# Position rows spread by SyncE one pair at a time, x in four buffers with its statistics on GpSimd, gate rows laid out by head: a change to a fused mLSTM and sparse-attention block

## The chip, the cores and the metric

The kernel runs on one core of a Trainium2 chip. A core has TensorE (PE), VectorE (DVE), ScalarE (ACT), GpSimd (POOL) and SyncE (SP), which here only issues transfers; 16 DMA engines move the data. The metric is the time of one execution in microseconds (us). Before the change it is 1576.97 us, the median of three runs (1576.12 to 1577.94).

## The reference, cut to what matters

One layer over 1024 positions of width 1024, in float32: a normalization, one input projection, two mixers side by side (an mLSTM with 4 heads of 128 and a sparse attention with 8 heads of 64 in 2 groups), gates that blend their outputs, an output projection, and a gated feed-forward network of width 2816.

```python
u = rms_norm(h, g_norm_mix[l])
proj = jnp.einsum('btd,de->bte', u, w_in[l]) + b_in[l]
mq, mk, mv, mo, mi, mf, nq, nkv, ngate, merge = split_columns(proj, IN_SIZES)
y_m = mlstm_mixer(mq, mk, mv, mo, mi, mf, ...)
y_n = nsa_mixer(nq, nkv, ngate, pe_cmp[l], w_cmp1[l], w_cmp2[l], rel_bias)
branch = jnp.einsum('btnw,nwd->btnd', jnp.stack([y_m, y_n], axis=2), w_branch[l])
h = h + jnp.sum(jax.nn.sigmoid(merge) * branch, axis=2) @ w_out[l]
f = rms_norm(h, g_norm_ffn[l])
h = h + (jax.nn.silu(f @ w_gate[l]) * (f @ w_up[l])) @ w_down[l]
```

`rms_norm` multiplies each row of x by the inverse root of its mean square. The mLSTM's gates `mi`, `mf` (8 columns of the projection) give, for each head and chunk of 128 positions, running sums, maxima and decays. The attention adds to its scores a bias `rel_bias` that depends on the distance between two positions only.

## The kernel before, in words

**Numbers.** Each float32 operand is split into a high part (f32r) and a low part (the rest), and each product is three matmuls: high × high, high × low, low × high (`mm3`, L289 to L292, so PE's rows have lines L290, L291, L292). ACT makes the high parts, VectorE or GpSimd the low ones by a subtraction (`ew`, L443 on GpSimd, L440 on VectorE; `act`, L447; `stt`, L450).

**The planner.** The first stage, to about 400 us, is not written in the order in which it runs. Its steps are given to a planner, `pA`, each with an engine, a cost in ns, the buffers it reads and writes, and sometimes an earliest time (`after`) or a rise in rank (`boost`). It builds one fixed order per engine ahead of the launch. The engines keep to their order and wait for each other by semaphores. So a changed cost can move many later instructions. SyncE issues its transfers in that order; each waits at its head of the queue until its buffers are free and until the eighth transfer before it has landed.

**The start (0 to 60 us).** x is loaded in eight tiles of 128 rows, in the order 0, 2, 4, 6, 1, 3, 5, 7 (XO), by `load_x` (L489) into slots of the buffer XR, three of them, x0 to x2; the fourth, x3, takes the junk output of ACT's Square. `norm` (L507) handles tile 0 alone and then the tiles in pairs, (2, 4), (6, 1), (3, 5) and 7: ACT squares and sums the row (L510), DVE forms mean plus epsilon (L511), ACT the root (L512), DVE the reciprocal and one Newton step of four operations (L516 to L520), and then DVE scales the tile (`stt`, L450, XR<-XR,MSC,PSA). `trans` transposes it on PE (L541) into UTH and UTL, and `p0` (L562) makes the first projection with the weights p0h, p0l (288 columns: values of the attention, into VT and VHA, and the gates, into GT, by a copy on GpSimd, L587). Meanwhile GpSimd loads rows of b_in into MSC, and stores the rows of bias by distance, d_row (8 heads of 1920 numbers).

**The pairs (60 to 330 us).** Twelve pairs of weight blocks (PAIRS, L720) are each multiplied by one level of Strassen's method, seven products instead of eight, in the order q = 1, 2, 6, 7, 5, 4, 3 (QO, L719). Weight blocks come by SyncE into rA and Rg; `prep` (L770) makes the sums of blocks (DVE L440, and rA, Rg as targets) and splits them into wOwhi and wOwlo; `product` (L864) is PE's part (PSA<-UTH,wOwhi and so on); `finish` (L802) adds products and bias into rows (DVE L450, RG or Rg), and `store` sends those to DRAM by SyncE (d_q<-Rg, d_kc<-Rg, 256 KB each). Rg and RG are used again and again, so a store must land before DVE writes its buffer anew. In front of the pairs stand `gates` (L945: maxima and decays of the mLSTM, small DVE and ACT operations, two transposes by way of DRAM, d_M and d_S, issued by GpSimd), and then eight loads on GpSimd's queue (L1144 and L1145), one for each attention head: each spreads one row of d_row over 128 rows of d_rep, from DRAM to DRAM, 960 KB. The attention reads d_rep only after 400 us. Their due times, 110 us and 14 us more for each, are the planner's; nothing on the chip holds them back.

**The mLSTM heads (280 to 400 us).** `head_load` (L1100) brings for each head the mask M, q, k, v, gate o and S into buffers, `values` (L1113) transposes v on PE (L1122), `core` (L1195) does the chunks.

**The branches (740 to 780 us).** For each of 8 column blocks two products with w_branch (L290 to L292, br<-YH,whi). The first weights are split on ACT (whi, L261) and DVE (wlo, L269). The sigmoid of the merge gates (L1866) is ACT's too, with a table load ahead of it. The inputs YH, YL are made tile by tile: DVE adds two halves (`split_y`, L1836), ACT and DVE split (L286, L287). FIRST (L1884) lists the first eight products; after the first, the second weight is split.

The rest, attention, output projection and feed-forward network (400 to 1578 us otherwise), is not touched.

Of the kernel before, what the change touches and what calls it, by code (L numbers as in the profile page):

```python
# [174 lines left out]
def body(ctx, tc, a, out, stop=None, dbg=None):  # L175
# [166 lines left out]
    with ExitStack() as sa:  # L342
# [119 lines left out]
        sq_A = K(sqA, keys=[("x3", 0)])  # L462
# [40 lines left out]
        def norm(*ii):  # L503
# [4 lines left out]
            for i in ii:  # L508
                sb_[i] = s
                stp("ACT", 1250.0, lambda i=i: nc.scalar.activation(sqA, flat(xb[i].ap), AF.Square, accum_out=stA[:, XO.index(i), 0:1]), [xb[i]], [s, sq_A])  # L510
            stp("DVE", 160.0, lambda: nc.vector.tensor_scalar(st[:, :, 0:1], st[:, :, 0:1], 1.0 / D, EPS, ALU.mult, ALU.add), (), [s])  # L511
            stp("ACT", 210.0, lambda: nc.scalar.activation(st[:, :, 1:2], st[:, :, 0:1], AF.Sqrt), tabs[-1:], [s])  # L512

            def newton():
# [5 lines left out]
                nc.vector.tensor_tensor(y, y, t, ALU.mult)  # L520
# [41 lines left out]
        def p0(i):  # L562
# [38 lines left out]
        def fsplit(q, j, src, reads):  # L601
# [168 lines left out]
        def prep(m, q):  # L770
# [150 lines left out]
        for n, i in enumerate(XO[4:]):  # L921
# [1614 lines left out]
```

## Time and profile before

| | us |
|---|---|
| median of three runs | 1576.97 |
| the profiled execution | 1580.19 |
| its span, first to last instruction | 1578.4 |
| PE busy | 1536.5 |
| DVE busy | 1153.7 |
| ACT busy | 793.3 |
| POOL busy | 174.4 |

The mean granted clock of TensorE was 0.989 of full speed. DMA moved 205.86 MB in 169979 packets. Rows of a timeline give the start in us, the duration, the engine (SPq is SyncE issuing a transfer), the line, the operation, output<-input, the shapes, how many were alike, and in brackets the idle time before with what ended it. Rows of waits give the engine and line that waited, the engine, buffer and line that released it, the us in all, the times and the longest. Rows of windows give start:end, length, the busy time of one or of each engine with its count of instructions, the granted clock, and what DMA did. The row PEclk gives the clock in tenths for 40 slices of the span.

### The profile page before, as it was taken

What the parts mean: (1) busy time and instruction counts of PE and PEld (TensorE: products, weight loads), DVE (VectorE), ACT (ScalarE), POOL (GpSimd) and SP (SyncE); (2) the same over time, 40 slices, a digit from 0 to 9 for tenths busy, and PEclk for the clock granted to TensorE, in tenths of its full rate; (3) what the DMA queues carried; (4) which work ended last, traced back from release to release, by engine and by line L of the source; (5) the groups of instructions that cost most, each with busy time, mean ns of one, the idle gap of its engine ahead of it and who ended that gap; (6) DMA issues with size and microseconds to landing.
All of it is one profiled execution on the core that took longest, in us unless ns stands there. A gap on an engine that the chain in (4) does not pass through costs nothing.

```text
span 1578.4 us, 22429 instructions
## 1 busy us (share of the span) xinstructions
PE 1536.5 (97%) x7810; PEld 1300.7 (82%) x7810; DVE 1153.7 (73%) x2380; ACT 793.3 (50%) x1713; POOL 174.4 (11%) x291
## 2 busy tenths in 40 slices
PE   9896999999999999999999999999999999999997
PEld 7775888888899989888788888888888888888886
DVE  5966788745798868784655677666666666988996
ACT  5533454457588868784444453333333333454443
POOL 4410001323111311002002000000000000000130
PEclk9997999999999999999999999999999999999999
DMA  6567455789523543216457324322222223750302
GB/s 201 170 185 225 125 173 166 201 259 190 179 53 103 99 111 71 83 48 236 144 161 226 107 81 134 94 80 81 81 87 87 80 80 113 274 193 22 107 0 107
DMA packets 169979, 205.86 MB, mean 130 GB/s; under 512 B 10345, under 2 KB 128391, under 8 KB 169610
## 3 DMA queue, kind: packets, MB, share of 16 engines
q1 hardware_dynamic: 156584, 179.43, 36.3%
q0 software_dynamic: 12992, 24.67, 6.8%
q8 instruction: 61, 1.00, 0.3%
q14 instruction: 52, 0.43, 0.1%
q10 hardware_dynamic: 290, 0.33, 0.1%
HBM read 149.77 MB, written 62.48 MB: 134 GB/s over the span
## 4 chain that ended last, share of the span: by engine, by line
PE 89%; DMA 5%; DVE 3%; ACT 1%; issue 1%; SPq 0%; POOL 0%; DVEq 0%; ACTq 0%; POOLq 0%
PE PS L291 14%; PE PS L290 14%; PE PS L292 14%; PE PSA L292 6%; PE PSA L290 6%; PE PSA L291 6%; PE T L1519 4%; PE d L290 3%; PE d L292 3%; PE d L291 3%; PE obank L1539 2%; PE obank L1541 2%; DMA d_q<-Rg 2%; PE br L292 2%; PE br L291 2%; PE br L290 2%
## 5 line engine op out<-in xcount | busy, mean ns | idle before, releaser
L1968 DVE TENSOR_TENSOR sl<-PS,sl 128x512 f32<-128x512 f32 x182 | 123.5, 688 | 100.9 <-PE PS L292 100.5
L1528 DVE TENSOR_TENSOR TL<-T,TH 128x512 fp32r<-128x512 f32 (+1 forms) x184 | 103.2, 581 | 32.5 <-ACT TH L1524 31.4
L1524 ACT ACTIVATE TH<-T 128x512 fp32r<-128x512 f32 (+1 forms) x184 | 90.1, 510 | 29.4 <-PE T L1519 26.8
L1968 DVE TENSOR_TENSOR sl<-sl,sl 128x512 f32<-128x512 f32 (+1 forms) x130 | 88.4, 687 | 22.0 <-DMA d_h<-sl 7.4
L292 PE MATMUL PSA<-UTH,wOwlo 128*128 128x512 f32 x164 | 65.2, 397 | 15.0 <-DVE wOwlo L440 15.0
L1971 ACT ACTIVATE sl<-sl 128x512 f32<-128x512 f32 (+1 forms) x77 | 48.6, 632 | 57.9 <-PE PS L291 34.4
L1968 POOL TENSOR_TENSOR acc<-acc 128x512 f32<-128x512 f32 x6 | 9.2, 1546 | 617.7 <-DVE acc L1968 617.6
L1539 PE MATMUL obank<-TH,VHL 128*128 128x256 f32 x264 | 75.4, 309 | 1.4 <-DMA VHL<-d_vh 1.4
L290 PE MATMUL d<-UTH,whi 128*128 128x512 f32 x176 | 71.9, 409 | 1.0 <-ACT mg L1355 0.7
L292 PE MATMUL d<-UTH,wlo 128*128 128x512 f32 x176 | 69.1, 393 | 0.0
L291 PE MATMUL d<-UTL,whi 128*128 128x512 f32 x176 | 69.0, 392 | 0.0
L1541 PE MATMUL obank<-TL,VHL 128*128 128x256 f32 x264 | 68.0, 281 | 0.0
L290 PE MATMUL PS<-q 128*128 128x512 f32 x172 | 66.9, 389 | 0.0
L291 PE MATMUL PS<-q 128*128 128x512 f32 x172 | 66.9, 389 | 0.0
L292 PE MATMUL PS<-q 128*128 128x512 f32 x172 | 66.9, 389 | 0.0
L1971 ACT ACTIVATE q<-sl 128x512 fp32r<-128x512 f32 x74 | 43.1, 623 | 42.3 <-PE PS L291 32.2
L290 PE MATMUL PSA<-UTH,wOwhi 128*128 128x512 f32 x156 | 63.4, 406 | 0.0
L291 PE MATMUL PSA<-UTL,wOwhi 128*128 128x512 f32 x156 | 60.8, 390 | 0.0
L1971 ACT ACTIVATE wh<-sl 128x512 fp32r<-128x512 f32 x39 | 24.6, 631 | 58.2 <-PE PS L291 40.8
L290 PE MATMUL br<-YH,whi 128*128 128x512 f32 x128 | 50.5, 395 | 2.2 <-ACT whi L261 2.2
L1539 PEld LDWEIGHTS obank<-TH,VHL 128*128 128x128 f32 x264 | 49.8, 189 | 2.6 <-ACT TH L1524 1.6
L292 PE MATMUL br<-YH,wlo 128*128 128x512 f32 x128 | 50.5, 395 | 0.5 <-DVE wlo L269 0.5
(1381 smaller groups left out, 4944.9 us busy)
## 6 DMA issues: line engine op xcount, KB each, us to landing
d_gu<-sl SPq DMA_DIRECT2D x44, 256.0 KB, 2.2
rA<-in_w_in SPq DMA_DIRECT2D x18, 512.0 KB, 5.9
q<-d_mg SPq DMA_DIRECT2D x32, 256.0 KB, 3.6
d_rep<-d_row POOLq DMA_DIRECT2D x8, 960.0 KB, 19.1
sl<-in_w_down SPq DMA_DIRECT2D x15, 512.0 KB, 3.4
sl<-d_gu SPq DMA_DIRECT2D x15, 512.0 KB, 4.7
ra<-in_w_gate SPq DMA_DIRECT2D x14, 512.0 KB, 3.8
ra<-in_w_up SPq DMA_DIRECT2D x13, 512.0 KB, 4.8
```

Source lines behind the costliest of these rows:

```text
L290: nc.tensor.matmul(ps, ah, bh, start=first, stop=False)
L291: nc.tensor.matmul(ps, ah, bl, start=False, stop=False)
L292: nc.tensor.matmul(ps, al, bh, start=False, stop=last)
L1519: nc.tensor.transpose(pt[:, z, P * r:P * r + P], e, ident)
L1524: nc.scalar.activation(hl[0][:, 0:m], pt[:, 0:m], AF.Copy)
L1528: nc.vector.tensor_tensor(hl[1][:, 0:m], pt[:, 0:m], cast32(hl[0])[:, 0:m], ALU.subtract)
L1539: nc.tensor.matmul(po, vv, th[:, z, :], start=(st[1] == 0), stop=False)
L1541: nc.tensor.matmul(po, vv, tl[:, z, :], start=False, stop=(st[1] == st[2]))
L1968: return pl.step(alts, lambda e: ENG[e].tensor_tensor(out_(), x(), y(), alu), reads, writes, **kw)
L1971: return pl.step((("ACT", cost),), lambda e: nc.scalar.activation(out_(), x(), fn), reads, writes, **kw)
```

## The change

**Broadcasts.** The eight loads of d_rep leave GpSimd's queue. SyncE issues one for each of the pairs m = 2 to 9, as a step behind the product (m, 7), and it counts as a reader of that product's weights, so the planner can't put it earlier than these are made.

**x and its statistics.** x has four slots, with two loads ahead instead of one; the junk output of Square goes to a PSUM bank, in two halves of 512 (for tile 0 still to x3). The mean (one small operation for tile 0, two otherwise) and the Newton step go to GpSimd; DVE keeps the reciprocal.

**Small shifts.** The low part of VHA is always GpSimd's, and that of the forms for q = 4, 5 may be; the first eight instead of four preps have a higher rank; one merge piece moves from x3 to x0.

**Layout by head.** Gate rows, maxima and decays are kept in the order head, chunk instead of chunk, head. The loads of M and S then read one contiguous row of 1024 numbers per head instead of eight pieces of 128. One copy of 32 numbers is added to `carry`.

**Heads and branches.** For heads 1 to 3, v is loaded first, then M, q, k. In the branch stage both first weights are fetched and split ahead of the first product, and the third is loaded there.

The diff, cut to its core (index changes of the layout by head are left out where they repeat):

```diff
         def load_x(i):
-            xb[i] = slot(f"x{XO.index(i) % 3}")
+            xb[i] = slot(f"x{XO.index(i) % 4}")
             load("SP", 512, [(lambda: flat(xb[i].ap), a["x"][P * i:P * i + P, :])], (), [xb[i]])
...
                 sb_[i] = s
-                stp("ACT", 1250.0, lambda i=i: nc.scalar.activation(sqA, flat(xb[i].ap), AF.Square, accum_out=stA[:, XO.index(i), 0:1]), [xb[i]], [s, sq_A])
-            stp("DVE", 160.0, lambda: nc.vector.tensor_scalar(st[:, :, 0:1], st[:, :, 0:1], 1.0 / D, EPS, ALU.mult, ALU.add), (), [s])
-            stp("ACT", 210.0, lambda: nc.scalar.activation(st[:, :, 1:2], st[:, :, 0:1], AF.Sqrt), tabs[-1:], [s])
+                if n == 0:
+                    junk = K(None, keys=[("x3", 0)], make=lambda: XR[:, 3, 0:512].bitcast(mybir.dt.bfloat16))
+                    stp("ACT", 1250.0, lambda i=i: nc.scalar.activation(junk.ap, flat(xb[i].ap), AF.Square, accum_out=st[:, 0, 0:1]), [xb[i]], [s, junk])
+                    continue
+                for z in range(2):
+                    junk = K()
+                    stp("ACT", 780.0, lambda i=i, z=z, junk=junk: nc.scalar.activation(junk.ap, xb[i].ap[:, z, :], AF.Square, accum_out=stA[:, XO.index(i), 3 * z:3 * z + 1]), [xb[i]], [s, junk])
+            y, v, g, w = (st[:, :, c:c + 1] for c in (2, 0, 3, 1))
+
+            def mean():
+                if n:
+                    nc.gpsimd.tensor_tensor(v, v, g, ALU.add)
+                nc.gpsimd.tensor_scalar(v, v, 1.0 / D, EPS, ALU.mult, ALU.add)
 
             def newton():
-                y, v, t = (st[:, :, n:n + 1] for n in (2, 0, 3))
-                nc.vector.reciprocal(y, st[:, :, 1:2])
-                nc.vector.tensor_tensor(t, y, y, ALU.mult)
-                nc.vector.tensor_tensor(t, t, v, ALU.mult)
-                nc.vector.tensor_scalar(t, t, -0.5, 1.5, ALU.mult, ALU.add)
-                nc.vector.tensor_tensor(y, y, t, ALU.mult)
-            stp("DVE", 950.0, newton, (), [s])
+                nc.gpsimd.tensor_tensor(g, y, y, ALU.mult)
+                nc.gpsimd.tensor_tensor(g, g, v, ALU.mult)
+                nc.gpsimd.tensor_scalar(g, g, -0.5, 1.5, ALU.mult, ALU.add)
+                nc.gpsimd.tensor_tensor(y, y, g, ALU.mult)
+            stp("Pool", 320.0, mean, (), [s])
+            stp("ACT", 210.0, lambda: nc.scalar.activation(w, v, AF.Sqrt), tabs[-1:], [s])
+            stp("DVE", 160.0, lambda: nc.vector.reciprocal(y, w), (), [s])
+            stp("Pool", 640.0, newton, (), [s])
...
-            if n + 3 < NT:
-                load_x(XO[n + 3])
+            if n + 4 < NT:
+                load_x(XO[n + 4])
...
         load_x(XO[3])
+        load_x(XO[4])
...
-            ew((("DVE", 430.0), ("Pool", 1000.0)), lambda: VHA[:, i, :, 64:128], lambda: vt, lambda: cast32(VHA)[:, i, :, 0:64], ALU.subtract, [vb], [hb])
+            ew((("Pool", 1100.0),), lambda: VHA[:, i, :, 64:128], lambda: vt, lambda: cast32(VHA)[:, i, :, 0:64], ALU.subtract, [vb], [hb])
...
-            ew(ANY if j < 2 else V, lambda: lo, src, lambda: cast32(hi), ALU.subtract, reads, [b])
+            ew(ANY if j < 2 or q in (4, 5) else V, lambda: lo, src, lambda: cast32(hi), ALU.subtract, reads, [b])
...
-            pA.boost = PB_ if nop[0] <= 4 else 0
+            pA.boost = PB_ if nop[0] <= 8 else 0
...
-            merge_half(0, z, mA, ("x3 g21".split()[z], 1), lambda n, z=z: [x for i in range(4 * z, 4 * z + 4) for x in (ub[i][0::2] if n >= 4 else ub[i][1::2])], fill=False)
+            merge_half(0, z, mA, ("x0 g21".split()[z], 1), lambda n, z=z: [x for i in range(4 * z, 4 * z + 4) for x in (ub[i][0::2] if n >= 4 else ub[i][1::2])], fill=False)
...
-            D_(200.0, lambda: nc.vector.tensor_copy(gif[:, 0], GT[:, :, 24:28]))
+            D_(200.0, lambda: nc.vector.tensor_copy(gif[:, 0].rearrange("p h c -> p c h"), GT[:, :, 24:28]))
...
-            P_(lambda: nc.tensor.transpose(pc.ap[0:32, 0:1], mp[:, 0:8, :].rearrange("p c h -> p (c h)"), ident[0:1, 0:1]), pc)
+                    nc.vector.tensor_tensor_scan(mp[:, h, 1:9], rw[:, 8 * h:8 * h + 8], rw[:, 32 + 8 * h:40 + 8 * h], 0.0, ALU.max, ALU.add)
+                nc.vector.tensor_copy(rw[:, 0:32].rearrange("p (h c) -> p h c", h=MH), mp[:, :, 0:8])
+            D2(1100.0, carry, pr)
+            P_(lambda: nc.tensor.transpose(pc.ap[0:32, 0:1], rw[:, 0:32], ident[0:1, 0:1]), pc)
 
             def maxima():
...
                 if key in "MS":
-                    r0 = (d_M if key == "M" else d_S)[h:h + 1, :]
-                    src = bass.AP(tensor=r0.tensor, offset=r0.offset, ap=[[0, P], [4 * P, NT], [1, P]])
-                    load("SP", 512, [(lambda b=b: v8c(b), src)], [b_MS], [b], cost=600.0)
+                    r0 = (d_M if key == "M" else d_S)[8 * h:8 * h + 1, :]
+                    src = bass.AP(tensor=r0.tensor, offset=r0.offset, ap=[[0, P], [1, T]])
+                    load("SP", 512, [(lambda b=b: flat(b.ap), src)], [b_MS], [b], cost=600.0)
...
-        for h in range(NH):
-            load("Pool", 983, [(d_rep[h], d_row[h, :].partition_broadcast(P))], (), [K(True)], cost=700.0, after=110000.0 + 14000.0 * h)
...
             product(m, q)
+            if q == 7 and 1 < m < NP - 2:
+                load("SP", 983, [(d_rep[m - 2], d_row[m - 2, :].partition_broadcast(P))], [OB[m, q]], [K(True)], cost=700.0)
...
-        head_load(1, "Mqkv")
+        head_load(1, "vMqk")
...
         for half in range(2):
             load_gates(1, half)
+        for d in range(2):
+            W[d] = ws.get(j_br[d])
+        ws.dma(j_br[2])
         for n, (d, half, b) in enumerate(FIRST):
-            if b == 0 and half == 0:
-                W[d] = ws.get(j_br[d])
             x = branch(d, half, b)
             if n == 0:
-                ws.split(j_br[1])
-                ws.dma(j_br[2])
                 gate(d, half, b, *x)
                 split_y(6)
                 continue```

SyncE's queue behind the gates, at pair 2, before (d_q, d_kc and d_mq are stores of results, rA, Rg and VW targets of loads):

```order
L416 DMA d_q_102<-RG_200 128x4x128
L416 DMA d_q_101<-RG_200 128x4x128
L416 DMA Rg_764<-in_w_in 128x4x256
L416 DMA d_kc_96<-RG_200 512x1x128
L416 DMA rA_206<-in_w_in 128x4x128 x2
L416 DMA d_kc_95<-RG_200 512x1x128
L416 DMA VW<-d_kc_95 64x1024
L416 DMA VW<-d_kc_95 64x1023
L416 DMA VW<-d_kc_95 64x1024
L416 DMA VW<-d_kc_95 64x1023
L416 DMA rA_207<-in_w_in 128x4x128 x2
```

and now:

```order
L415 DMA d_q_102<-RG_200 128x4x128
L415 DMA d_rep_84<-d_row 128x1920
L415 DMA d_q_101<-RG_200 128x4x128
L415 DMA Rg_791<-in_w_in 128x4x256
L415 DMA d_kc_96<-RG_200 512x1x128
L415 DMA d_kc_95<-RG_200 512x1x128
L415 DMA rA_206<-in_w_in 128x4x128 x2
L415 DMA VW<-d_kc_95 64x1024
L415 DMA VW<-d_kc_95 64x1023
L415 DMA VW<-d_kc_95 64x1024
L415 DMA VW<-d_kc_95 64x1023
L415 DMA d_rep_85<-d_row 128x1920
```

The first broadcast stands between two stores of d_q and the second ahead of the next weight loads; the other six follow 7 to 18 transfers apart.

GpSimd's queue at the start now (MSC holds the statistics, p0l the low part of the first weights, RG the raw ones):

```order
L520 TENSOR_SCALAR MSC<-MSC 128x1
L523 TENSOR_TENSOR MSC<-MSC 128x1
L524 TENSOR_TENSOR MSC<-MSC 128x1
L525 TENSOR_SCALAR MSC<-MSC 128x1
L526 TENSOR_TENSOR MSC<-MSC 128x1
L566 TENSOR_TENSOR p0l<-RG_200,p0h 128x576 x2
L415 DMA MSC<-in_b_in 128x128
L415 DMA MSC<-in_b_in 128x152
L415 DMA MSC<-in_b_in 128x8
L519 TENSOR_TENSOR MSC<-MSC 128x2
L520 TENSOR_SCALAR MSC<-MSC 128x2
L415 DMA d_row<-ewwlo_211 8x480
```

Before, p0l was GpSimd's first arithmetic, and the three loads of b_in were followed by two stores of d_row; now tile 0's statistics stand ahead of p0l, and the mean of the pair (2, 4) behind the loads.

ACT's queue at the first branch products, before (q are gates and halves of y, d a merge gate's product, whi the second weight's high part):

```order
L1355 ACTIVATE q_5_0_7735<-d_1_7880,COLS 128x512
L1866 ACT_TABLE_LOAD
L1866 ACTIVATE q_3_4_7747<-q_3_4_7747 128x512
L261 ACTIVATE whi_7934<-raw_7835 128x1024
L286 ACTIVATE YH<-q_0_2_7745 128x512 x2
```

and now:

```order
L1366 ACTIVATE q_5_0_7757<-d_1_7902,COLS 128x512
L261 ACTIVATE whi_7942<-raw_7857 128x1024
L1877 ACT_TABLE_LOAD
L1877 ACTIVATE q_3_4_7769<-q_3_4_7769 128x512
L286 ACTIVATE YH<-q_0_2_7767 128x512 x2
```

The split of the second weight has moved from behind the table load and the first sigmoid to ahead of both.

More of the change, by code (lines that the diff above doesn't have):

```diff
@@ L360, in body @@
         stA = MSC[:, 680:712].rearrange("p (i c) -> p i c", i=NT)
-        gif = MSC[:, 712:776].rearrange("p (z c h) -> p z c h", z=2, c=NT)
+        gif = MSC[:, 712:776].rearrange("p (z h c) -> p z h c", z=2, c=NT)
         rw = MSC[0:1, 776:840]
-        mp = MSC[0:1, 840:876].rearrange("p (c h) -> p c h", c=9)
+        mp = MSC[0:1, 840:876].rearrange("p (h c) -> p h c", c=9)
         stage = RG0.rearrange("p (k c) -> p k c", k=KT)
@@ L461, in body @@
         GPRIOR = {"0": b_st, "1": b_p0h, "2": b_p0l}
-        sq_A = K(sqA, keys=[("x3", 0)])
         xform, b_rr, b_vh = [], [], []
@@ L965, in gates @@
             pg, pr, pc, pq = (K() for _ in range(4))
-            D_(200.0, lambda: nc.vector.tensor_copy(gif[:, 0], GT[:, :, 24:28]))
+            D_(200.0, lambda: nc.vector.tensor_copy(gif[:, 0].rearrange("p h c -> p c h"), GT[:, :, 24:28]))
             pA.todo["DVE"][-1].deps |= set(b_GT.w) | {b_rows[7].w[0]}
-            D_(200.0, lambda: nc.vector.tensor_tensor(gif[:, 1], GT[:, :, 28:32], BF[:, None, :].to_broadcast([P, NT, MH]), ALU.add))
+            D_(200.0, lambda: nc.vector.tensor_tensor(gif[:, 1].rearrange("p h c -> p c h"), GT[:, :, 28:32], BF[:, None, :].to_broadcast([P, NT, MH]), ALU.add))
             for z in range(2):
-                P_(lambda z=z: nc.tensor.transpose(pg.ap[0:32, P * z:P * z + P], gif[:, z].rearrange("p c h -> p (c h)"), ident), pg)
+                P_(lambda z=z: nc.tensor.transpose(pg.ap[0:32, P * z:P * z + P], gif[:, z].rearrange("p h c -> p (h c)"), ident), pg)
             iT, fT = t(), t()
@@ L1000, in carry @@
                 nc.vector.tensor_copy(rw, pr.ap[0:1, 0:64])
-                nc.vector.memset(mp[:, 0, :], 0.0)
+                nc.vector.memset(mp[:, :, 0:1], 0.0)
                 for h in range(MH):
-                    nc.vector.tensor_tensor_scan(mp[:, 1:9, h], rw[:, h:32:4], rw[:, 32 + h:64:4], 0.0, ALU.max, ALU.add)
-            D2(1000.0, carry, pr)
-            P_(lambda: nc.tensor.transpose(pc.ap[0:32, 0:1], mp[:, 0:8, :].rearrange("p c h -> p (c h)"), ident[0:1, 0:1]), pc)
+                    nc.vector.tensor_tensor_scan(mp[:, h, 1:9], rw[:, 8 * h:8 * h + 8], rw[:, 32 + 8 * h:40 + 8 * h], 0.0, ALU.max, ALU.add)
+                nc.vector.tensor_copy(rw[:, 0:32].rearrange("p (h c) -> p h c", h=MH), mp[:, :, 0:8])
+            D2(1100.0, carry, pr)
+            P_(lambda: nc.tensor.transpose(pc.ap[0:32, 0:1], rw[:, 0:32], ident[0:1, 0:1]), pc)
             def maxima():
@@ L1211, in st_a @@
                 E_, PT[c], KW[c] = take("E"), take("PT"), take("KW")
-                stp("ACT", 400.0, lambda: nc.scalar.activation(E_.ap, v8(MB)[:, c, :], AF.Exp, bias=GCOL[:, 4 * c + h:4 * c + h + 1]), [MB, b_gc, tabs[-1]], [E_])
+                stp("ACT", 400.0, lambda: nc.scalar.activation(E_.ap, v8(MB)[:, c, :], AF.Exp, bias=GCOL[:, 8 * h + c:8 * h + c + 1]), [MB, b_gc, tabs[-1]], [E_])
                 stp("DVE", 290.0, lambda: nc.vector.tensor_tensor(PT[c].ap, pa_.ap[:, 0:128], E_.ap, ALU.mult), [pa_, E_], [PT[c]])
@@ L1234, in st_b @@
                     else:
-                        stt(350.0, lambda: CN.ap, lambda: CN.ap, DEC[:, 4 * c + h:4 * c + h + 1], lambda: o(pu), ALU.mult, ALU.add, [pu, b_dec], [CN])
+                        stt(350.0, lambda: CN.ap, lambda: CN.ap, DEC[:, 8 * h + c:8 * h + c + 1], lambda: o(pu), ALU.mult, ALU.add, [pu, b_dec], [CN])
                 stp("ACT", 290.0, lambda: nc.scalar.activation(nd[:, c, :], o(pn), AF.Copy), [pn], [ndb])
@@ L1255, in norm_1 @@
                 nc.vector.scalar_tensor_tensor(t0, den, -1.0, den, ALU.mult, ALU.max)
-                nc.vector.tensor_tensor(t0, t0, ECOL[:, h:32:4], ALU.max)
+                nc.vector.tensor_tensor(t0, t0, ECOL[:, 8 * h:8 * h + 8], ALU.max)
                 nc.vector.reciprocal(t0, t0)
@@ L1301, in body @@
         core(0)
-        head_load(2, "Mqkv")
+        head_load(2, "vMqk")
         mask(2)
@@ L1308, in body @@
         core(1)
-        head_load(3, "Mqkv")
+        head_load(3, "vMqk")
         mask(3)
```

1 line of the change is left out of this document (removed).

## The prediction

> **What bounds the kernel now.** I read the page of the profile first: the busy shares and the row of granted clocks.
>
> ```profile
> PE 1536.5 (97%) x7810; PEld 1300.7 (82%) x7810; DVE 1153.7 (73%) x2380; ACT 793.3 (50%) x1713; POOL 174.4 (11%) x291
> ...
> PEclk9997999999999999999999999999999999999999
> ```
>
> TensorE (PE) is busy for 1536.5 of 1578.4 us, and the change takes no matmul away. All it can win is the 41.9 us in which PE is idle, and the time in which PE runs at a lowered clock (the 7, slice 4, 118 to 158 us, is such a place). So next I read what PE waited for in four windows: 0 to 50 us, 50 to 140, 330 to 450 and 740 to 765. Each row gives the us in all, the count and the longest.
>
> ```profile
> PE PSA L541 <- DVE XR L450: 4.7, 1, 4.7
> ...
> PE PSA L292 <- DVE wOwlo L440: 15.8, 2, 15.0
> ...
> PE PSA L1122 <- DMA XB<-d_mv: 2.9, 1, 2.9
> ...
> PE br L290 <- ACT whi L261: 2.2, 1, 2.2
> PE br L292 <- DVE wlo L269: 0.5, 1, 0.5
> ```
>
> One wait of 15.0 us is over a third of all idle time. The change touches all of these places, and I take them one by one.
>
> **The stall at 115 us: eight broadcasts d_rep.** The queues of GpSimd and SyncE, VectorE's and PE's timelines, the busy times in VectorE's gap, and the DMA queues and issues from 98 to 131 us:
>
> ```profile
> 98.16 3.59 POOL L416 DMA_DIRECT2D d_rep<-d_row  x7
> ...
> 100.09 1.50 SPq L416 DMA_DIRECT2D d_q<-Rg  x2
> ...
> 128.96 0.75 DVE L450 SCALAR_TENSOR_TENSOR Rg<-PSA,COLS,XR 128x512 f32<-128x512 f32 x1 [21.71 <-DMA d_q<-Rg]
> ...
> 130.36 0.79 PE L292 MATMUL PSA<-UTH,wOwlo 128*128 128x512 f32 x1 [14.98 <-DVE wOwlo L440]
> ...
> 107.26:128.96 21.70, 8.12 (x36) 6.38 (x34) 0.00 (x1) 0.00 (x1) 0.00 (x0) 0.77 1.01 308
> ...
> q0 software_dynamic: 1232, 7.88, 77.3%
> ...
> d_q<-Rg SPq DMA_DIRECT2D x2, 256.0 KB, 17.5
> ```
>
> GpSimd issues seven broadcasts within 3.6 us. From then on their queue fills 77.3% of 16 engines for 33 us: 0.773 × 33 / 8 = 3.2 us of all engines for each. Behind them two stores of 256 KB, issued from 100.1 on, take 17.5 us. VectorE must not write Rg again before its store has landed; it comes for it at 128.96 - 21.71 = 107.25 and stands still. PE works on for 8.1 us (the window's first number after its length), runs dry, and waits 14.98 us. After that it works at half clock (us; PE busy; clock; DMA share; GB/s):
>
> ```profile
> 130.40:136.00 5.60, 5.60 (x13) 0.50 1.03 323
> 136.00:141.60 5.60, 5.60 (x26) 1.00 0.59 147
> ```
>
> 13 matmuls in 5.6 us and then 26 in the next 5.6: 2.8 us more are lost.
>
> In the changed program no broadcast stands in GpSimd's queue here. SyncE issues the first behind those stores, and the others one a pair, 7 to 18 of its transfers apart. So the store should take what an undisturbed one of its size takes:
>
> ```profile
> d_gu<-sl SPq DMA_DIRECT2D x44, 256.0 KB, 2.2
> ```
>
> Issued at 100.1 to 101.6, it lands by 104, before VectorE wants Rg. What is late next? Nothing that the rows show: in the gap VectorE, ACT and GpSimd did nothing at all, and a shorter wait is covered by PE's 8.1 us of lead. I take 14.98 + 2.8 = **17.8 us** gained; bounds 15 (the clock falls anyway) and 18.6 (the small waits of that window go too, 15.8 in all).
>
> **What the broadcasts cost where they go.** PE, PEld, DVE, ACT, POOL, clock, DMA share and GB/s from 140 to 330 us, and PE, clock, share and GB/s in the fullest part:
>
> ```profile
> 140.00:330.00 190.00, 190.00 (x880) 158.36 (x879) 147.41 (x204) 86.47 (x144) 23.95 (x30) 1.00 0.60 168
> ...
> 280.00:320.00 40.00, 40.00 (x178) 1.00 0.84 217
> ```
>
> PE never waits there, and on average 40% of DMA time is free. One broadcast every 20 us or so adds 3.2 / 20 = 0.16 to the share, which just fits even at 0.84. Behind each on SyncE's own queue stand the next stores and weight loads. How much delay such a store bears can be read off the stall: issued at 101, wanted at 107.25, usual time 2.2, so 4 us spare, and PE's lead of 8.1 after that: 12 us against 3.2. I cost the eight at **0**. A gain is excluded, since PE has no wait to lose there; the bounds are 0 and 8 × 3.2 = 25.6 (rival c).
>
> [...]
>
> **The start: four x buffers, statistics on GpSimd.** PE, ACT, DVE and POOL before 60 us:
>
> ```profile
> 24.86 0.38 PE L290 MATMUL PSA<-p0h,UTH 128*128 128x288 f32 x1
> ...
> 31.55 2.63 PE L541 MATMUL PSA<-cst,XR 128*128 128x128 f32 x16
> 33.93 0.38 PE L290 MATMUL PSA<-p0h,UTH 128*128 128x288 f32 x1
> ...
> 45.66 3.67 PE L541 MATMUL PSA<-cst,XR 128*128 128x128 f32 x16 [4.68 <-DVE XR L450]
> ...
> 56.20 0.60 PE L541 MATMUL PSA<-cst,XR 128*128 128x128 f32 x4
> ...
> 40.57 1.06 ACT L510 ACTIVATE XR<-XR 128x1024 bf16<-128x1024 f32 x1 [2.91 <-DMA XR<-in_x]
> ...
> 19.75 0.17 DVE L520 TENSOR_TENSOR MSC<-MSC 128x2 f32<-128x2 f32 x1
> 19.95 1.41 DVE L450 SCALAR_TENSOR_TENSOR XR<-XR,MSC,PSA 128x512 f32<-128x512 f32 x2
> ...
> 18.60 1.65 POOL L416 DMA_DIRECT2D MSC<-in_b_in  x3
> ...
> 23.15 0.21 POOL L587 COPY GT<-VT 128x32 f32<-128x32 f32 x1 [1.07 <-DVE VT L586]
> ...
> 58.38 0.49 POOL L587 COPY GT<-VT 128x32 f32<-128x32 f32 x1
> ```
>
> Gain: with three buffers x5 arrives late, ACT's Square of it waits until 40.57, and PE waits 4.68 us for x3 and x5, which are normalized together. With a fourth buffer, and the loads ahead of a weight load, this wait goes. Loss: x2 and x4 are normalized later. Their mean now stands on GpSimd behind three DMA issues that end at 20.25, after which come 2 + 4 small GpSimd operations, a root on ACT, a reciprocal on DVE and four changes of engine. Small GpSimd arithmetic isn't in the trace of before; its nearest rows are the 128x32 copies, 0.21 us and, when the engines are full, 0.49. I take 0.21, the row nearest in time: 6 × 0.21 + 2 × 0.17 (root and reciprocal, by VectorE's row at 19.75) + 4 × 0.25 (my estimate of a change of engine) = 2.6. So scaling starts at 22.8 rather than 19.95, and allowing 0.4 us that PE fills, x2's projection at 27.3 rather than 24.86. From there I lay PE's rows end to end. Two projections take 6.7 (24.86 to 31.55): x4's ends at 34.0. About 1.3 us idle before x6's transposes, since its scaling moves as well, and 2.63 + 0.7 for these: 38.6 (33.93 before). x6's and x1's projections took from 33.93 to 40.98 (45.66 - 4.68), 7.05: 45.65. Then, without a wait, 2.63 for the transposes of x3 and x5 and 6.7 for their projections: 55.0, where before stands 56.20: **+1.2**. The new idle time may bring a half-clock stretch, which cost 2.8 above; I don't count on one, since PE's longest new idle time is 1.3 us. Bounds: six operations at 0.49 for each of two more pairs, exposed, 2 × 1.7 = 3.4 worse: -3; the wait of 4.7 won with the lag hidden: +5.
>
> Lower parts that go from VectorE to GpSimd (VHA, some forms) unload the engine that PE waited for at 45.66; 0. The layout by head adds one copy of 32 elements off PE's path; 0.
>
> **Head 1's v.** SyncE's queue, landing times, PE's timeline and the chain of waits at 330 us:
>
> ```profile
> 326.14 0.58 SPq L416 DMA_DIRECT2D XB<-d_M  x1
> ...
> XB<-d_M SPq DMA_DIRECT2D x1, 512.0 KB, 7.4
> ...
> 331.00 0.27 PE L1209 MATMUL PSA<-cst,VW 128*128 128x128 f32 x1
> ...
> 327.98 10.33 DMA XB<-d_mv
> ...
> 338.44 1.06 PE PSA L1122 x8
> ```
>
> v was issued fourth, at 327.98, and took 10.33. Now it is first, at about 326.1, where d_M took 7.4. A store of half its size takes 2.2, so 4.4 would be the least; I take the middle, 5.9: landing at 332.0. PE's order also asks for v earlier, in place of the block that ends at 331.1, so 0.9 to 1.0 of the 2.9 remains: **+1.9**; bounds 0.5 and 2.9.
>
> **The branch stage.** ACT, DVE and PE's clock at 755 us:
>
> ```profile
> 752.55 1.28 ACT L1866 ACT_TABLE_LOAD   x1 [3.95 <-DMA q<-d_mg]
> ...
> 754.38 1.04 ACT L261 ACTIVATE whi<-raw 128x1024 fp32r<-128x1024 f32 x1
> ...
> 760.92 1.22 DVE L1836 TENSOR_TENSOR q<-q 128x1024 f32<-128x1024 f32 x1
> ...
> 757.20:760.60 3.40, 3.40 (x10) 0.50 0.55 163
> ```
>
> The second weight's split on ACT stood behind a table load that waits for the gates until 752.55; now it stands ahead of it, in ACT's 3.95 us of idle time. That wins 2.16 (its row above, 2.2) + 0.53 and the half clock of 757.2 to 760.6, 1.7. Next to be late is the last tile of y, whose sum (760.92) is still behind the first two gates: with PE some 3 us earlier I put the new wait at 0.9. **+3.5**; bounds 1.8 (the clock falls all the same) and 4.4.
>
> **Sum.** 17.8 + 0 + 1.2 + 1.9 + 3.5 = 24.4 us. The span of 1578.4 becomes 1554.0. The profiled execution, 1580.2, is 1.8 above its span and 3.2 above the median of the runs shown (1576.97), and the gain is taken off that median: 1552.6.
>
> **Rivals.**
> (a) The start turns out worse: GpSimd's small operations at 0.49, -3 for +1.2: 1556.8. With one or two broadcasts exposed as well, 3.2 to 6.4: 1560 to 1563. For it: the row of 58.38. Against: GpSimd is 11% busy.
> (b) Half the stall stays. Not the broadcasts alone, but SyncE's own loads and stores hold the store up: it lands late, VectorE waits, and 8.9 of 17.8 are won: 1561.5. Against: to cost PE anything the store would have to land after 115, 14 us after its issue.
> (c) Slower: the broadcasts stand in the one queue that brings weights and takes results away. If each holds back what the next products need by all its 3.2 us, and PE idles each time, 25.6 are lost: 1578.2; with half clock after each wait (8 × 1.7), 1591.8. It decides from 24.4 / 8 = 3.05 us exposed a pair. For it: the share of 0.84 at the end. Against: the 12 us of slack and lead. [...]
> (d) The start wins its whole wait: +5 for +1.2, and the last 0.9 in the branch stage: 1547.9.
> (e) The change doesn't do as it says, and the planner bunches the broadcasts again: SyncE's order shows them apart, so no chance.
>
> **Chances.** The forecast, 1549 to 1556.5: 0.6; (a) 0.17; (b) 0.08; (c) 0.06; (d) 0.09. The range reaches to the far side of (d) and through (a) to (b): 1547 to 1564. A measurement of this kernel can tell about 0.2%, 3.2 us, from no change. Faster 0.93: all but (c) and a little of (b). Within it 0.03: (c) at the strength that just eats the gain. Slower 0.04: (c) in full.
>
> **What would show it.** Right: VectorE without a wait on d_q from 100 to 130 us; PE busy at full clock from 60 to 330 us; broadcasts that land in 4 to 9 us each; no wait of 4.7 at x3's transposes, but x2's projection 2 to 3 us later; whi ahead of the table load. Wrong: PE waits for weights or stores next to a d_rep, or half clock after 140 us (c); GpSimd's statistics at 0.5 us, PE idle from 20 to 40 us (a); VectorE waiting on Rg at 107 us again (b).

## The result

The changed kernel takes 1555.86 us, the median of four runs (1554.76 to 1556.88), beside 1577.45 for the kernel before in the same comparison (four runs, 1576.12 to 1578.2): 21.6 us less. The ratio is 0.9864, with a 95% interval of 0.9847 to 0.9881, which is 18.8 to 24.1 us. The profiled execution took 1556.88 with a span of 1555.1, so by the two spans (1578.4 before) the gain is 23.3.

The page of the profile after, busy shares and granted clock:

```profile
PE 1533.9 (99%) x7810; PEld 1299.3 (84%) x7810; DVE 1149.2 (74%) x2351; ACT 793.7 (51%) x1724; POOL 191.9 (12%) x330
...
PEclk8999999999999999999999999999999999999999
```

PE's idle time went from 41.9 to 21.2 us. Its busy time fell by 2.6 us with the same 7810 matmuls, as less of it runs at half clock: the 7 in the row of clocks is gone, and the mean clock is 0.995, where it was 0.989. PE's waits over the whole span, us in all, times, longest:

```profile
PE PSA L550 <- ACT VHA L446: 1.7, 1, 1.7
PE PSA L550 <- DVE XR L449: 1.3, 1, 1.3
PE PSA L292 <- DVE wOwhi L439: 1.2, 1, 1.2
PE obank L1550 <- DMA VHL<-d_vh: 1.2, 1, 1.2
PE PSA L580 <- ACT p0h L446: 1.2, 2, 0.9
PE PSA L498 <- DVE MSC L367: 1.1, 1, 1.1
PE PSA L290 <- ACT wOwhi L446: 0.8, 1, 0.8
...
PE br L290 <- ACT YH L286: 0.6, 1, 0.6
```

The waits of 15.0, 4.7, 2.9 and 2.2 us are gone; nothing longer than 1.7 has come. The first two rows stand at new places, and the third and seventh (1.2 and 0.8, at 75 to 78 us) are new. DMA from 98 to 131 us, where the broadcasts had filled the engines: queues, and issues with KB and us to landing:

```profile
q1 hardware_dynamic: 8499, 7.14, 79.9%
q0 software_dynamic: 144, 0.05, 3.0%
...
d_rep<-d_row SPq DMA_DIRECT2D x2, 960.0 KB, 6.5
...
d_q<-RG SPq DMA_DIRECT2D x4, 256.0 KB, 4.0
d_q<-Rg SPq DMA_DIRECT2D x2, 256.0 KB, 3.6
```

The stores of d_q land in 3.6 to 4.0 us instead of 17.5 (not the 2.2 that I took, but before VectorE wants their buffers: it no longer waits for a store between 100 and 135 us), and two of the eight broadcasts fall into this window instead of all.

To see where the time went I follow four landmarks on PE that both programs have: x7's transposes (56.20 before), the first transposes of head 0's v, the first attention product, and the first and last branch product. Before:

```profile
L1122 PE MATMUL PSA<-cst,Rg x16: 271/272/273, 328.6 to 361.1; 128*128 128x128 f32 x16
...
L1539 PE MATMUL obank<-TH,VHL x264: 275/282/387, 415.6 to 723.0; 128*128 128x256 f32 x132
...
L290 PE MATMUL br<-YH,whi x128: 389/389/628, 747.7 to 838.9; 128*128 128x512 f32 x128
```

and after (each row gives ns min/median/max and the first and last start):

```profile
54.14 0.39 PE L290 MATMUL PSA<-UTH,wOwhi 128*128 128x512 f32 x1
...
55.52 0.60 PE L550 MATMUL PSA<-cst,XR 128*128 128x128 f32 x4
...
L1133 PE MATMUL PSA<-cst,Rg x16: 271/272/273, 311.4 to 342.9; 128*128 128x128 f32 x16
...
L1550 PE MATMUL obank<-TH,VHL x264: 277/282/387, 395.6 to 703.0; 128*128 128x256 f32 x132
...
L290 PE MATMUL br<-YH,whi x128: 389/389/502, 727.7 to 815.6; 128*128 128x512 f32 x128
```

| stretch | before | after | difference | forecast |
|---|---|---|---|---|
| start, to x7's transposes | 56.2 | 55.5 | -0.7 | -1.2 |
| pairs, to head 0's v | 272.4 | 255.9 | -16.5 | -17.8 |
| heads, to the first attention product | 87.0 | 84.2 | -2.8 | -1.9 |
| attention, to the first branch product | 332.1 | 332.1 | 0 | 0 |
| branch products | 91.2 | 87.9 | -3.3 | -3.5 |
| the rest | 739.5 | 739.5 | 0 | 0 |

The first landmark has moved in PE's order. Six matmuls of the first pair, 1.4 us (54.14 to 55.52), now run ahead of x7's transposes; before, none did. By equal work the start has gained 2.1 us and the pairs 15.1.

### The profile page after: what moved, and what is told of

Same layout as the page of the kernel before. It is cut to its first block, busy times and chain, and to the rows that moved or that the text cites. A ratio compares the mean times of both kernels' runs of the same rounds, so it can differ in the third digit from the quotient of the medians.

```text
span 1555.1 us, 22464 instructions
## 1 busy us (share of the span) xinstructions
PE 1533.9 (99%) x7810; PEld 1299.3 (84%) x7810; DVE 1149.2 (74%) x2351; ACT 793.7 (51%) x1724; POOL 191.9 (12%) x330
## 4 chain that ended last, share of the span: by engine, by line
PE 90%; DVE 4%; DMA 3%; ACT 1%; issue 1%; POOL 0%; SPq 0%; DVEq 0%; POOLq 0%; ACTq 0%
PE PS L291 15%; PE PS L290 15%; PE PS L292 15%; PE PSA L290 6%; PE PSA L292 6%; PE PSA L291 6%; PE T L1530 4%; PE d L290 2%; PE obank L1550 2%; PE d L292 2%; PE d L291 2%; PE obank L1552 2%; PE br L291 2%; PE br L292 2%; PE br L290 2%; DVE acc L1978 1%
## 5 line engine op out<-in xcount | busy, mean ns | idle before, releaser
L1539 DVE TENSOR_TENSOR TL<-T,TH 128x512 fp32r<-128x512 f32 (+1 forms) x184 | 103.1, 581 | 32.5 <-ACT TH L1535 31.4
L1550 PE MATMUL obank<-TH,VHL 128*128 128x256 f32 x264 | 75.5, 309 | 1.2 <-DMA VHL<-d_vh 1.2
L290 PE MATMUL d<-UTH,whi 128*128 128x512 f32 x176 | 71.9, 409 | 1.0 <-ACT mg L1366 0.7
L292 PE MATMUL d<-UTH,wlo 128*128 128x512 f32 x176 | 69.1, 393 | 0.0
L290 PE MATMUL PS<-q 128*128 128x512 f32 x172 | 66.9, 389 | 0.0
L292 PE MATMUL PS<-q 128*128 128x512 f32 x172 | 66.9, 389 | 0.0
L290 PE MATMUL PSA<-UTH,wOwhi 128*128 128x512 f32 x156 | 64.6, 414 | 0.8 <-ACT wOwhi L446 0.8
L292 PE MATMUL PSA<-UTH,wOwlo 128*128 128x512 f32 x164 | 64.1, 391 | 0.0
L267 POOL TENSOR_TENSOR wlo<-raw,whi 128x256 fp32r<-128x256 f32 x44 | 32.1, 759 | 168.6 <-ACT whi L261 138.3
L1550 PEld LDWEIGHTS obank<-TH,VHL 128*128 128x128 f32 x264 | 49.8, 189 | 2.4 <-ACT E1c L1479 1.4
L1552 PEld LDWEIGHTS obank<-TL,VHL 128*128 128x128 f32 x264 | 50.0, 189 | 1.1 <-DVE TL L1539 0.3
## 6 DMA issues: line engine op xcount, KB each, us to landing
d_gu<-sl SPq DMA_DIRECT2D x44, 256.0 KB, 2.2
q<-d_mg SPq DMA_DIRECT2D x32, 256.0 KB, 3.1
```

The costliest lines, as they stand in the source:

```text
L267: nc.gpsimd.tensor_tensor(lo[:, zs], v[:, zs], cast32(hi)[:, zs], ALU.subtract)
L290: nc.tensor.matmul(ps, ah, bh, start=first, stop=False)
L292: nc.tensor.matmul(ps, al, bh, start=False, stop=last)
L1539: nc.vector.tensor_tensor(hl[1][:, 0:m], pt[:, 0:m], cast32(hl[0])[:, 0:m], ALU.subtract)
L1550: nc.tensor.matmul(po, vv, th[:, z, :], start=(st[1] == 0), stop=False)
L1552: nc.tensor.matmul(po, vv, tl[:, z, :], start=False, stop=(st[1] == st[2]))
```

## The experiments

My theory: the stall came from eight broadcasts in flight at once, and one at a time is hidden; the places are independent. Rivals: it is the queue that counts, not the spacing; a broadcast on SyncE's queue costs something each time; the start is no gain. Ratios are to the kernel before in the same session; its median there was 1580.1 to 1580.9 (1575.3 to 1584.9).

**Broadcasts back on GpSimd, all else as in the changed kernel.**

```diff
-            if q == 7 and 1 < m < NP - 2:
-                load("SP", 983, [(d_rep[m - 2], ...)], [OB[m, q]], [K(True)], cost=700.0)
+        for h in range(NH):
+            load("Pool", 983, [(d_rep[h], ...)], (), [K(True)], cost=700.0, after=110000.0 + 14000.0 * h)
```

> The changed kernel with only the eight broadcasts back on GpSimd's queue, all issued behind the gates. Theory (the stall comes from eight broadcasts in flight at once): VectorE waits some 20 us on a store of d_q again, PE idles 13 to 16 us near 115 us, and the time is 1555.9 + 16 to 18 = 1572 to 1574. Rival (the stall went because the planner reordered the work around it, not because of the broadcasts): no such wait, within 3 us of 1555.9.

1572.59 us, ratio 0.996 (0.9943 to 0.9977). The stall is back: PE's waits from 60 to 160 us, and VectorE's.

```profile
PE PSA L292 <- DVE wOwlo L439: 15.1, 1, 15.1
PE PSA L292 <- DVE wOwhi L439: 1.2, 1, 1.2
PE PSA L290 <- ACT wOwhi L446: 0.8, 1, 0.8
```

```profile
DVE RG L449 <- DMA d_q<-RG: 22.5, 1, 22.5
```

This time it is the buffer RG rather than Rg, of a later store, with the same effect. The stretch of the pairs takes 271.3 us (324.3 less 52.96), 15.4 more than in the changed kernel. So the new order of the work around it is not what removed the stall.

**Only the spread, in the kernel before.** The edit is the reverse, on the kernel before.

> The kernel before with only the broadcasts moved to SyncE, one a pair; start, heads and branches as before. Theory: the gain of the whole change less the start (0.7), heads (2.8) and branches (3.3): 1577.5 - 16 to 18 = 1559.5 to 1561.5, with the waits of 4.7 at x3, 2.9 at head 1's v and 2.7 in the branches still there. Rival (the spread needs the earlier start and the new ranks to be hidden): PE waits beside a broadcast after 130 us, 1564 or more.

1562.53 us (1 us above the range expected), ratio 0.9906 (0.9875 to 0.9937); by the interval 10 to 20 us faster. PE's waits, up to 60 us and at the heads:

```profile
PE PSA L541 <- DVE XR L450: 3.9, 1, 3.9
...
PE PSA L1122 <- DMA XB<-d_mv: 2.7, 1, 2.7
```

Start and heads wait as before, and no wait stands beside a broadcast. The pairs take 255.3 us (307.8 less 52.47), 17.1 less than before: the spread does it alone.

**The same spacing on GpSimd's queue.** The planner's claim that a broadcast reads the product's weights makes no semaphore, since the transfer doesn't read them; on GpSimd's queue, which is otherwise empty from 103 to 246 us, it would pace nothing. So a copy that does read them stands ahead of each:

```diff
             if q == 7 and 1 < m < NP - 2:
-                load("SP", 983, ...)
+                stp("Pool", 150.0, lambda m=m, o=OB[m, q]: nc.gpsimd.tensor_copy(PACE[0:1, m:m + 1], cast32(o.ap[:, 0, :])[0:1, 0:1]), [OB[m, q]], [K(True)])
+                load("Pool", 983, ...)
```

> The changed kernel with the broadcasts on GpSimd's queue, but paced: ahead of each stands a copy of one number that reads the weights of the product (m, 7), so GpSimd issues it only when these are made. Theory (only the spacing counts, not the queue): no stall, 1555.9 within 2 us. Rival (a queue of its own is what hurts, since its packets take turns with SyncE's): waits of a store of some us beside each broadcast, 1560 to 1572. Second rival (SyncE's one ring costs something in the changed kernel): 1 to 5 us faster, 1551 to 1555.

1555.59 us (1553.61 to 1556.04), ratio 0.9853 (0.983 to 0.9876): as the changed kernel. That the packets of two queues take turns is in the trace of the kernel before: from 104 to 126 us, 988 packets of GpSimd's queue (6.74 MB) and 979 of SyncE's (0.49 MB) ran. At this spacing that costs nothing that can be measured. GpSimd's issues, the first two, and the landing of all eight:

```profile
112.43 0.55 POOL L416 DMA_DIRECT2D d_rep<-d_row  x1
131.06 0.52 POOL L416 DMA_DIRECT2D d_rep<-d_row  x1
```

```profile
d_rep<-d_row POOLq DMA_DIRECT2D x8, 960.0 KB, 5.0
```

The pairs take 255.8 us against 255.9. At this spacing it makes no difference whether a broadcast lands in 5.0 us on a queue of its own or in 6.9 (all eight) on SyncE's. What the change got from SyncE's queue is the pace, without an instruction for it.

**All eight at one place on SyncE's queue.** The step of the change, with all eight broadcasts behind the product (2, 7).

> The changed kernel with all eight broadcasts on SyncE's queue at pair 2, between three transfers of results, instead of one a pair. Theory (bunching is the cause in any queue, and in one ring the transfers behind have to wait for all of them): 8 x 3.2 = 25.6 us of transfers ahead of the next loads and stores, less some 12 us of slack and lead: PE idle 12 to 20 us, 1568 to 1579. Rival (SyncE's queue protects the stores by its order): 1556 to 1559.

1561.1 us, ratio 0.9897 (0.9869 to 0.9924). Neither number came out: the pairs take 260.4 us (315.1 less 54.69), only 4.5 more than spread. SyncE's queue and PE's waits from 100 to 140 us:

```profile
109.44 0.92 SPq L415 DMA_DIRECT2D d_q<-RG  x2
110.52 1.86 SPq L415 DMA_DIRECT2D d_rep<-d_row  x3
112.49 0.65 SPq L415 DMA_DIRECT2D d_q<-RG  x1
113.18 1.25 SPq L415 DMA_DIRECT2D d_rep<-d_row  x2
115.91 0.57 SPq L415 DMA_DIRECT2D d_kc<-RG  x1
116.53 5.36 SPq L415 DMA_DIRECT2D d_rep<-d_row  x3
124.93 0.39 SPq L415 DMA_DIRECT2D Rg<-in_w_in  x1
```

```profile
PE PSA L290 <- ACT wOwhi L446: 2.2, 1, 2.2
PE PSA L292 <- DVE wOwhi L439: 0.7, 1, 0.7
```

The stores ahead of them are safe, and what was pushed back (the next weights, issued at 124.9 rather than 117.6) costs PE 2.9 us of waits and some half clock behind them (a clock of 0.91 from 120 to 140 us). So bunching costs 15 us where the broadcasts start at 98 to 100 us, ahead of stores that are wanted 6 us after their issue, and 4.5 where they start at 110, behind most of these. Whether it is SyncE's queue or the place that helped is not told apart by these runs.

**Each broadcast twice, and four times.**

```diff
-                load("SP", 983, [(d_rep[m - 2], d_row[m - 2, :].partition_broadcast(P))], ...)
+                load("SP", 983, [(d_, d_row[m - 2, :].partition_broadcast(P)) for d_ in (d_rep[m - 2], *d_more[m - 2])], ...)
```

> The changed kernel with each broadcast issued twice on SyncE, the second into memory that nobody reads. Theory (a broadcast is covered by the slack of some 12 us): 3.2 us more of DMA time a pair, 114 + 51 of 190 us, so no wait of PE: 1555.9 within 1.5. Rival (the transfers behind are on the path): up to 8 x 3.2 = 25.6 more, and at least 5: 1561 to 1581.

1555.24 us, ratio 0.9839 (0.9822 to 0.9856): nothing.

> The changed kernel with each broadcast issued four times. From 140 to 330 us the DMA engines were 0.60 busy without any (114 us); 8 x 12.8 = 102 us on top is 216 in 190. Theory (slack up to the capacity of the DMA engines, then the excess shows): 10 to 35 us more, 1566 to 1591, with PE waits from the later pairs on. Rival (much more slack than 12 us a pair, since weights are loaded far ahead): under 5 us more. Rival (already past the edge): over 40 more.

1580.97 us, ratio 1.0007 (0.9996 to 1.0018). PE, clock, DMA share and GB/s from 140 to 300 us in the changed kernel, with two and with four:

```profile
140.00:300.00 160.00, 160.00 (x741) 1.00 0.70 207
```

```profile
140.00:300.00 160.00, 160.00 (x742) 1.00 0.80 245
```

```profile
140.00:300.00 160.00, 144.11 (x636) 0.95 0.97 299
```

At a share of 0.80 PE still has no idle time; at 0.97 it has 15.9 us, and its mean clock is 0.95. The pairs take 280.2 us, 24.3 more, near the 26 of the count 216 less 190. So the broadcasts are hidden until the DMA engines are full, and the rival of 3 us exposed a pair is far off: at twice the load it costs nothing. What stands behind a broadcast on SyncE's queue does wait for it: in the changed kernel a store of d_q was issued at 113.53 us, behind the broadcast of 112.86, and from 114.75 to 117.5 us the queue ran 99 packets of 7680 bytes, a row of the broadcast each, and none of the store's 512. That costs nothing that can be measured here up to the doubled load: what waits behind a broadcast has more slack than the broadcast is long.

**Statistics back on VectorE.** In `mean` and `newton`, nc.gpsimd becomes nc.vector, and "Pool" becomes "DVE".

> The changed kernel with the mean and the Newton step on VectorE again, as before; four buffers and all else kept. Theory (the hops to GpSimd delay the pair 2, 4 by some 2 to 3 us, which the removed wait pays back): PE starts the projection of x2 some 2 us earlier and the whole is 1 to 2 us faster than 1555.9. Rival (VectorE is the bound of the start, so its small operations cost more there): 0 to 2 us slower.

1556.4 us (1551.46 to 1556.83), ratio 0.9844 (0.9829 to 0.9859). By the median there is no difference that could decide between the two. The profiled execution, 1551.46, is the fastest of the five by 3 us, and in it the start does run ahead as the theory had it: x7's transposes begin at 54.41 rather than 55.52, with 15 product matmuls ahead of them rather than 6. Why the other four runs don't show this stays open, as they left no trace.

**Forms back as before.** One line:

```diff
-            ew(ANY if j < 2 or q in (4, 5) else V, lambda: lo, src, lambda: cast32(hi), ALU.subtract, reads, [b])
+            ew(ANY if j < 2 else V, lambda: lo, src, lambda: cast32(hi), ALU.subtract, reads, [b])
```

> The changed kernel with the low parts of the forms for q = 4 and 5 as before (GpSimd only for the first two blocks). In the changed kernel PE waits 0.8 and 1.2 us at 75 to 78 us, where VectorE's operations from SBUF to SBUF take 1.1 to 2.3 us rather than 0.68 while GpSimd works beside them. Theory (GpSimd's share slows VectorE): these waits shrink and the time falls by 1 to 2 us, to 1554 to 1555. Rival (VectorE's load is what counts): the waits there grow, 1 to 3 us slower, 1557 to 1559.

1552.64 us (1551.46 to 1553.98), ratio 0.9822 (0.9807 to 0.9837), some 3 us better than the changed kernel, where 1 to 2 were expected. PE, PEld, DVE, ACT, POOL, clock, DMA share and GB/s from 60 to 82 us, of this kernel:

```profile
60.00:82.00 22.00, 21.52 (x103) 17.54 (x102) 21.83 (x37) 13.11 (x24) 7.82 (x10) 1.00 0.63 219
```

and of the changed kernel:

```profile
60.00:82.00 22.00, 19.95 (x91) 16.29 (x90) 21.83 (x29) 12.01 (x21) 13.70 (x16) 0.92 0.56 199
```

In the same 21.83 us of busy time VectorE gets 37 operations done, not 29. VectorE's timeline of the changed kernel, and then GpSimd's, show why:

```profile
65.90 0.68 DVE L439 TENSOR_TENSOR RG<-PSA,RG 128x512 f32<-128x512 f32 x1
66.50 0.68 DVE L439 TENSOR_TENSOR RG<-RG,UTL 128x512 f32<-128x512 f32 x1
...
68.54 2.33 DVE L439 TENSOR_TENSOR RG<-RG,UTL 128x512 f32<-128x512 f32 x1
```

```profile
68.87 1.44 POOL L442 TENSOR_TENSOR UTL<-RG,UTH 128x256 fp32r<-128x256 f32 x2
```

The same operation takes 0.68 us, and 2.33 beside two of GpSimd's; one with PSUM as one source, RG<-PSA,RG at 67.10, keeps its 0.68 beside GpSimd's operations for VHA. At 66.50 it was GpSimd that came second: these two operations, from 66.51, take 1.42 us, where such a pair took 0.88 at 36.13. The pairs take 252.6 us (306.7 less 54.06), 3.3 less than in the changed kernel, with the same six matmuls ahead. By the time alone this would not be sure, since the interval overlaps those of the doubled broadcasts and of the statistics on VectorE, from the same session. The traces say it again. With the matmuls ahead of x7's transposes counted in (0.23 us each), the pairs take 254.0 us here and 254.8 in the variant with forms and statistics on VectorE, but 256.2 to 257.3 in four kernels with the forms on GpSimd (the changed one, paced, doubled, statistics on VectorE).

**Heads and branches alone, in the kernel before.**

```diff
-        head_load(1, "Mqkv")
+        head_load(1, "vMqk")
...
+        for d in range(2):
+            W[d] = ws.get(j_br[d])
+        ws.dma(j_br[2])
```

> The kernel before with only two edits: v loaded first for heads 1 to 3, and both first branch weights split ahead of the first product. Theory (the places are independent, each worth what it showed): the wait of 2.9 at head 1's v falls under 0.5 and the waits of 2.2 and 0.5 in the branches go; 2.8 + 3.3 = 6.1 us faster than before, a ratio of 0.996. Rival (the gain at head 1's v came from the stall being gone, which shifted the DMA traffic): v lands late again, 1 to 3 us less gain, 0.997 to 0.998.

1573.76 us, ratio 0.9961 (0.9945 to 0.9976), the 0.996 expected. By landmarks the branch products take 88.1 us (-3.1); the heads 85.7 (-1.3), where v lands in time, in 4.2 us, but a new wait for ACT takes part of it. That makes 4.4 of the 6.1 expected, inside the interval of the ratio (3.8 to 8.7 us). The heads gained 2.8 in the whole change; what else there is in it is not separated. The layout by head, which I had costed at 0, was not tried alone: with it M lands in 5.3 us, here in 7.3.

```profile
PE PSA L1208 <- ACT XR L1236: 1.6, 1, 1.6
```

**The start alone, in the kernel before.** Four buffers, statistics on GpSimd, Square into PSUM banks, VHA.

> The kernel before with only the start's edits: four x buffers, statistics on GpSimd, Square into PSUM banks, low part of VHA on GpSimd. Theory (the wait of 4 to 5 us goes, but 2 to 3 us of lag come back, and what is left is under what runs differ by): a ratio of 0.998 to 1.001, x7's transposes at 53 to 55 us. Rival (the start is a gain of its own, as the sum had it, with the half clock after the wait): 1.2 to 5 us, 0.997 to 0.999, x7's transposes before 53.

1578.43 us, ratio 0.9995 (0.9981 to 1.0008); x7's transposes at 53.11: both as the theory had them. No gain can be measured, but by the interval one of up to 3.0 us is not excluded either.

**Forms and statistics both back on VectorE.** The two edits above together.

> The changed kernel with the forms' low parts and the statistics both back on VectorE; four buffers, spread broadcasts, heads and branches kept. Theory (the forms' return is worth 3 us, the statistics' nothing): as with the forms alone, ratio 0.982 within 0.001. Rival (GpSimd's lag at the start is worth its 2 us as well): 0.9805 or less.

1552.22 us, ratio 0.9827 (0.981 to 0.9844), as with the forms alone. With that, the best version is the change without its line on the forms; GpSimd's statistics can stay or go.

**The kernel before, a second time.**

> The kernel before, unchanged, profiled a second time. Theory (its first profile was 3 us above the median because of half clock after the wait of 4.7 us, which comes in some runs only): x7's transposes at 52 to 54 us rather than 56.2, the stall of 15 us as it was, a span of 1574 to 1576. Rival (the first profile is typical): 56 and 1578.

1580.06 us, span 1578.3. PE's timeline at x3 and x7:

```profile
45.03 3.11 PE L541 MATMUL PSA<-cst,XR 128*128 128x128 f32 x16 [3.62 <-DVE XR L450]
55.25 0.60 PE L541 MATMUL PSA<-cst,XR 128*128 128x128 f32 x4
```

Only the stall came out as the theory had it, 15.1 us. For the rest the rival was right, with x7's transposes at 55.25 and a span of 1578.3: the first profile is typical, and its late start is no single accident. With the old start, x7's transposes stood at 56.20, 55.25, 52.47 and 51.53 in four profiles, and the wait at x3 was 4.7, 3.6, 3.9 and 3.0 us.

## Why the prediction was right, point by point

The time came out at 1555.9 where 1552.6 was forecast, within the range, and the mechanism of the main term was right: the chain from broadcasts to a store, to VectorE, to PE.

- **The stall, 17.8.** The spread alone is worth 17.1 (in the kernel before) and 15.4 (in the changed one), both within the bounds of 15 to 18.6. The stretch of the pairs gained 15.1 by equal work, as what the lower parts cost (below) comes off it.
- **The broadcasts where they go, 0.** Right, and with much to spare: twice the load costs nothing. The slack of 12 us a pair that I read off the stall was too careful (how much lead the weights have of their own, no run measures); what ended it was that the DMA engines were full, at a share of 0.97 with four times the load. Full clock from 60 us on, which I gave as a sign, did not come: 0.87 from 70 to 80 us, for the reason that follows.
- **Lower parts from VectorE to GpSimd, 0.** This step failed. I wrote that they unload the engine that PE waits for, and gave no price to the two engines getting in each other's way. It costs 3.3 us in the pairs, as new waits of 0.8 and 1.2 us and time at half clock behind them; where no half clock followed (a clock of 1.00 from 70 to 90 us), 1.4 (252.7 with the statistics on VectorE, 251.3 with the forms there too).
- **The start, +1.2.** The sizes were good: GpSimd's small operations took 0.18 to 0.21 us, all but two of 0.5 to 0.6, and x2's scaling began at 22.91 (22.8 forecast). But this is in part luck. The change of engine, at 0.25 us an estimate with no row behind it, shows as 0.03: the mean ends at 20.54 on GpSimd, ACT's root runs from 20.57 to 20.78, and VectorE's reciprocal starts at 20.81. The Newton step was done at 22.23, and what the scaling stood behind at last was VectorE's VT, which waited for b_in (GpSimd's timeline, then VectorE's):

```profile
22.03 0.20 POOL L526 TENSOR_TENSOR MSC<-MSC 128x2 f32<-128x2 f32 x1
```

```profile
22.53 0.46 DVE L595 TENSOR_TENSOR VT<-PSA,MSC 128x288 f32<-128x288 f32 x1 [1.55 <-DMA MSC<-in_b_in]
22.91 2.71 DVE L449 SCALAR_TENSOR_TENSOR XR<-XR,MSC,PSA 128x512 f32<-128x512 f32 x4
```

x7's transposes came at 55.52 (55.0 forecast), with six matmuls ahead that the sum did not have: 54.1 by equal work, a gain of 2.1. But the 56.20 that I took them from was the latest of four profiles of the old start (mean 53.9), and eight of the new start with GpSimd's statistics average 54.1, 52.7 by equal work. That is 1.2 us between averages of profiles that spread over 4.7 and 2.6 us, and the ratio of 0.9995 can't tell it from nothing: that it meets the forecast is luck. The old wait of 4 us is traded for two new ones (1.7 and 1.3), the lag, and a half clock that I did not count on: 0.66 from 20 to 30 us, where the profile before had 1.00.
- **Head 1's v, +1.9.** 2.8: v landed in 4.3 us, the lower bound of my 4.4 to 7.4, so nothing was left of the wait. With the reordering alone the heads gained 1.3, so the 2.8 are not shown to be v's.
- **The branches, +3.5.** 3.3, with the new wait for the last tile of y that was forecast at 0.9: 0.6 and 0.2.
- **The base.** By spans 24.4 was forecast and 23.3 measured. By equal work the pairs fell short by 2.7, the start and the heads each won 0.9 more, the branches 0.2 less. The medians differ by 21.6, since the profiled execution before lay 2.7 above its median and that after 1.0. I took off the median of three runs a sum made in an execution 3.2 above it. In the later sessions the median of before is 1580.1 to 1580.9, so the profile was no outlier; the first few runs lie low against these. Of the 3.3 us between forecast and result, 1.1 come from the terms and 2.2 from the base.

The rivals: (b) had no part in it. (c) fell with the doubled broadcasts. (d) fell with the start. (a) named 1556.8, near the result, but by another cause: only two of GpSimd's small operations took over 0.5 us, and what the terms fell short by, 1.1, lies in the pairs, where the forms cost more than that.

## What to carry to other kernels

Bulk transfers with no due time belong where a queue paces them. Eight in flight at once cost 15 us through one store of 256 KB whose buffer was wanted 6 us after its issue, while one at a time cost nothing that these runs can tell, on either queue, and on SyncE's not even two at a time; four filled the DMA engines (a share of 0.97) and cost 24.3 us in the pairs. Before small VectorE work is moved to GpSimd, look at what runs beside it: here an operation with both inputs in SBUF took 2.33 us instead of 0.68, so a move can cost the busy engine more than it takes off it.

## What the runs showed of the hardware

The half clock after short waits comes in one execution and not in another. The kernel before, profiled twice, ran from 15 to 25 us at 1.00 in one and at 0.71 in the other. In the changed kernel and in the one with the broadcasts back on GpSimd, PE stood still for 2.05 us in the same stretch of 10 us (us; PE busy; clock; DMA share; GB/s), first the changed one:

```profile
70.00:80.00 10.00, 7.95 (x30) 0.87 0.60 236
```

```profile
70.00:80.00 10.00, 7.95 (x34) 1.00 0.35 123
```

The first got four matmuls fewer done. Two waits of 2.05 us together (0.8 and 1.2) were followed by the half clock in the one and not in the other, and waits of 2.2 and 0.5 us in the branches of the kernel before were followed by it too (0.50 from 757.2 to 760.6 us). What decides whether it comes, these runs don't show. So a wait of some 2 us should be priced with and without its half clock.
